# Moving the norm sums, the GpSimd passes and the attention transposes of a two-block fp32 network on one Trainium2 core

## The chip, the cores and the metric

The kernel runs on one core of one Trainium2 chip. The metric is the device time of one execution in microseconds (us), from the first to the last instruction with what the runtime adds around it. TensorE does the matrix products (its weight loads are listed apart, as PEld), VectorE (DVE) and ScalarE (ACT) do elementwise work and reads of PSUM, GpSimd (POOL) does some elementwise passes that touch no PSUM, and SyncE (SP) starts most of the DMAs.

## What is computed

Two blocks run on a sequence of 512 tokens of width 1024, in fp32. The first block is a mixer (a gated MLP branch and a linear recurrence with forget gates, called HGRN2, joined by gates and an output product), followed by a feed-forward part with squared ReLU. The second block has two layers; each is a gated feed-forward part (GLU), a mixer, and another GLU. The mixer of layer 0 is differential attention beside a multiscale pool, the mixer of layer 1 is a short causal convolution. Each part begins with a norm over the 1024 features of a token:

```python
def rmsnorm_2(x, g):
    xf = x.astype(jnp.float32)
    y = xf * lax.rsqrt(jnp.mean(xf * xf, axis=-1, keepdims=True) + EPS)
    return (y * g.astype(jnp.float32)).astype(x.dtype)

def modulated_norm(x, g, shift, scale):
    return rmsnorm_2(x, g) * (1 + scale) + shift

def swiglu(h, wg, wu, wd):
    return (jax.nn.silu(h @ wg) * (h @ wu)) @ wd
```

The shift and scale of the second block come from a vector `c` through a large matrix `w_ada` (72 DMAs of 1 MB). One norm, after the first block, is two norms in a row (its final norm and the first norm of the second block).

## The kernel before, in words

**Layout.** Activations are kept with the features on the 128 partitions and the tokens along the free axis: x is eight tiles of 128x512 (`xs(m)`). A product in fp32 is made of three passes in the faster format fp32r (`mm3`, L135): each operand is split into a high and a low part (`split`, L201; `wblock`, L119, for weights: ACT writes `whi` at L128, DVE writes `wlo` at L129), and high by high, high by low and low by high are added in PSUM (L139, L140, L141). Weights come in 1 MB DMAs on SP's queue; two landing buffers and four pairs of `whi`/`wlo` are in rotation.

**A norm between two parts.** `down` (L291) makes the last product of a part, feature tile by feature tile. After each tile it updates x on DVE (L300 or L298), squares it on ACT (L220) and adds the square into the sum `SS` (L226; on POOL for all tiles but the last). For the last two tiles (m = 6 and 7) the tokens go in two halves of 256. From here on the order of TensorE's instructions is the written one (`order_pe`), to the end of the next part's first products (`free_pe`); the other engines are ordered by the scheduler when the kernel is built. `norm_parts` (L249) gives two pieces per half. `sums` adds over the partitions with a matmul (L232), makes mean plus epsilon on DVE (L94) and raises it to -1/2 on POOL (L95). `tiles` spreads the 256 results over all partitions (`bcast`, L97) and then makes the eight normed tiles: `ht` on DVE (L270), its high part on ACT (L274 or L277), its low part on DVE (L275 or L278). `bcast` splits the two columns into high and low (L100, L101, both DVE), writes them into a diagonal matrix (L104, DVE, 512 columns for the two parts) and multiplies it by ones (L111, two fp32r matmuls of 256 columns).

In the order of TensorE the first half's `sums` stand just after the product of tile 6, second half; then comes the product of tile 7, second half, and the first half's spread stands three of its steps before the end:

```python
        finish(6, self.gemm([ws[0]], xs, 256, 256)[0], 1)
        parts[0][0]()
        n = len(xs)
        ps = self.acc()
        for k in range(n):
            if k == n - 3 and pre is None:
                parts[0][1]()
            self.mm3(ps, ws[1], k, xs[k], 256, 256, k == 0, k == n - 1)
```

In the double norm (`pre`) both sums are taken and the spread comes after the whole product. There are seven such norms; six of them are plain.

**First products of a part.** `lead_gemm` (L363) multiplies the first half of the tokens by four weight units at once, so that each normed tile feeds 12 matmuls of 256 columns; after the second and the fifth tile it puts the second half's `sums` and spread (`pump`). `lead_second` (L372) then does the second half, two units at a time. This is used by the feed-forward with ReLU, by four GLUs and by the convolution (L1084); attention has its own form by tokens (`gemm_tok_halves`, L180).

**Other passes on POOL.** The sums of squares of the first norm (L403), the affine part of a layer norm (L671, L672), the sum of the two gated branches (L539), the output gate of the recurrence (L642), the windows of the pool (L919) and the first tap of the convolution (L1097). The small powers (L95) are on POOL too.

**Attention.** `attn` (L809) makes q and k by tokens, norms them per head (`qk_evac`: square on ACT, L853 and L856 on DVE, power on POOL) and turns them (`finish`, L868 transposes). Then 16 steps run (token block i, head h), each in stages that belong to different steps: stA scores and exponentials, stB two steps later (difference of the two softmaxes, transposes at L984), stC three steps later (product with v at L993, norm, L996, L95, L999), stD four steps later (transpose at L1006, write of `oT`). Between the stages TensorE is filled with products for v and for the pool (`fill`), and after the last step with the beginning of the output product (`opening`), which needs the pool's results `pT`. `pool_out` multiplies a pool window by a 128x128 matrix that POOL's queue loads just before (L941, L942). The order of TensorE is the written one here too.

## Time and profile before

| | us |
|---|---|
| three runs | 2772.61, 2772.81, 2776.55 |
| median | 2772.81 |
| profiled execution | 2773.61 |
| its span | 2771.8 |
| mean granted TensorE clock | 0.991 of 2.4 GHz |

In a row of the timeline stand the start, the duration, the engine, the source line, the operation, what is written from what, the number of merged instructions, and in brackets how long the engine had been idle and for what. A matmul's duration holds its passage through the array, which overlaps the next one; how long a matmul costs is read from the distance of two starts. "PE acc L140 <- DVE h L275" says that a matmul of L140 waited for the DVE instruction of L275.

### The profile page before, as it was taken

To read this page: it belongs to the slowest core of one execution; us is meant where nothing else is said; L and a number is where in the kernel's file an instruction comes from. 1 tells how busy PE (TensorE), PEld (TensorE's weight loads), DVE (VectorE), ACT (ScalarE), POOL (GpSimd) and SP (SyncE) were. 2 spreads that over 40 slices of the span, in tenths; PEclk is the share of its full clock that TensorE was granted. 3 is DMA by queue.
4 is the path that set the end of the run, shared out by engine and by line. 5 is a ranking of instruction groups with operands and counts; after the bars stand their busy time and mean duration, and the time that the engine had idled before them with its cause. 6 is when DMAs were issued, how large, how long until landed. Compare 5 with 4: busy or idle time off the path is not lost.

```text
span 2771.8 us, 32091 instructions
## 1 busy us (share of the span) xinstructions
PE 2709.4 (98%) x13188; PEld 2279.7 (82%) x13188; DVE 1417.9 (51%) x2220; ACT 857.1 (31%) x1279; POOL 222.5 (8%) x205
## 2 busy tenths in 40 slices
PE   8999999999999899999989999999999999999999
PEld 6888888888888788887768888888888888888888
DVE  7566643476556755557567333354333354533333
ACT  5222232333224322224444222233222332332221
POOL 3000010200002000002221000010000111100000
PEclk9999999999999999999999999999999999999999
DMA  4211133355555455543223222322323222232222
GB/s 156 77 63 59 39 122 107 115 199 188 198 191 183 151 193 199 197 180 129 77 79 137 92 101 89 103 88 92 106 84 107 99 77 94 89 107 92 99 102 73
DMA packets 51266, 327.97 MB, mean 118 GB/s; under 512 B 5824, under 2 KB 6464, under 8 KB 17072
## 3 DMA queue, kind: packets, MB, share of 16 engines
q1 hardware_dynamic: 50256, 323.11, 33.0%
q0 software_dynamic: 864, 2.82, 0.3%
q8 instruction: 103, 1.69, 0.2%
q14 instruction: 43, 0.35, 0.0%
HBM read 323.81 MB, written 2.10 MB: 118 GB/s over the span
## 4 chain that ended last, share of the span: by engine, by line
PE 88%; DVE 6%; DMA 3%; issue 1%; POOL 1%; ACT 1%; SPq 0%; DVEq 0%; POOLq 0%; ACTq 0%
PE acc L140 26%; PE acc L141 26%; PE acc L139 26%; DMA ada<-in_w_ada 2%; PE ms L585 2%; DVE ada L784 1%; DVE wlo L129 1%; PE acc L172 1%; PE acc L173 1%; PE acc L171 1%; PE ms L623 1%; PE acc L199 0%; PE acc L197 0%; PE acc L198 0%; PE ms L111 0%
## 5 line engine op out<-in xcount | busy, mean ns | idle before, releaser
L128 ACT CAST whi<-w 128x1024 fp32r<-128x1024 f32 (+1 forms) x468 | 481.9, 1030 | 1517.5 <-PE acc L140 1407.5
L139 PE MATMUL acc<-h,whi 128*128 128x512 f32 (+1 forms) x2352 | 892.9, 380 | 3.8 <-ACT h L277 2.5
L140 PE MATMUL acc<-h,whi 128*128 128x512 f32 (+1 forms) x2352 | 887.4, 377 | 3.5 <-DVE h L275 2.6
L141 PE MATMUL acc<-h,wlo 128*128 128x512 f32 (+1 forms) x2352 | 885.9, 377 | 1.1 <-DVE wlo L129 1.1
L129 DVE TENSOR_TENSOR wlo<-w,whi 128x1024 fp32r<-128x1024 f32 (+1 forms) x468 | 573.4, 1226 | 447.5 <-ACT whi L128 439.0
L140 PEld LDWEIGHTS acc<-h,whi 128*128 128x128 f32 x2352 | 446.8, 190 | 83.8 <-DVE h L275 3.4
L139 PEld LDWEIGHTS acc<-h,whi 128*128 128x128 f32 x2352 | 446.9, 190 | 83.2 <-ACT h L277 3.6
L141 PEld LDWEIGHTS acc<-h,wlo 128*128 128x128 f32 x2352 | 446.4, 190 | 79.4 <-DVE wlo L129 1.7
L139 PE MATMUL acc<-y,whi 128*128 128x512 f32 (+1 forms) x1112 | 415.0, 373 | 1.0 <-ACT y L204 1.0
L140 PE MATMUL acc<-y,whi 128*128 128x512 f32 (+1 forms) x1112 | 414.8, 373 | 1.1 <-DVE y L205 1.1
L141 PE MATMUL acc<-y,wlo 128*128 128x512 f32 (+1 forms) x1112 | 414.7, 373 | 0.0
L784 DVE SCALAR_TENSOR_TENSOR ada<-ada,cb 128x1024 f32<-128x1024 f32 x144 | 181.6, 1267 | 118.6 <-DMA ada<-in_w_ada 118.2
L140 PEld LDWEIGHTS acc<-y,whi 128*128 128x128 f32 x1112 | 209.7, 189 | 38.4 <-DVE y L205 1.8
L139 PEld LDWEIGHTS acc<-y,whi 128*128 128x128 f32 x1112 | 209.7, 189 | 38.0 <-ACT y L204 1.4
L141 PEld LDWEIGHTS acc<-y,wlo 128*128 128x128 f32 x1112 | 209.7, 189 | 36.3
L300 DVE SCALAR_TENSOR_TENSOR xt<-acc,dmod,xt 128x512 f32<-128x512 f32 (+1 forms) x124 | 86.6, 698 | 261.4 <-PE acc L141 261.3
L764 DVE TENSOR_TENSOR e<-acc,e 128x512 f32<-128x512 f32 (+1 forms) x92 | 60.4, 656 | 233.3 <-PE acc L141 232.9
L204 ACT CAST y<-e 128x512 fp32r<-128x512 f32 (+1 forms) x140 | 81.6, 584 | 69.2 <-DVE e L749 38.4
L205 DVE TENSOR_TENSOR y<-e,y 128x512 fp32r<-128x512 f32 (+1 forms) x140 | 89.5, 640 | 11.0 <-ACT y L204 10.9
L223 POOL COPY SS<-sq 128x512 f32<-128x512 f32 x8 | 7.2, 912 | 995.6 <-ACT sq L220 995.6
L226 POOL TENSOR_TENSOR SS<-SS,sq 128x512 f32<-128x512 f32 x40 | 63.9, 1601 | 109.6 <-ACT sq L220 107.6
L277 ACT ACTIVATE h<-ht,mod 128x256 fp32r<-128x256 f32 x96 | 44.6, 502 | 75.3 <-DVE ht L270 75.3
(268 smaller groups left out, 2234.7 us busy)
## 6 DMA issues: line engine op xcount, KB each, us to landing
w<-in_w_gu SPq DMA_DIRECT2D x88, 1024.0 KB, 4.8
ada<-in_w_ada SPq DMA_DIRECT2D x72, 1024.0 KB, 6.3
w<-in_w_ff SPq DMA_DIRECT2D x32, 1024.0 KB, 4.8
w<-in_w_dn SPq DMA_DIRECT2D x32, 896.0 KB, 4.6
w<-in_w_dn SPq DMA_DIRECT2D x16, 1024.0 KB, 4.8
w<-in_w_fq SPq DMA_DIRECT2D x8, 1024.0 KB, 4.7
w<-in_w_gg SPq DMA_DIRECT2D x8, 1024.0 KB, 5.7
w<-in_w_cx SPq DMA_DIRECT2D x8, 1024.0 KB, 4.8
```

Source lines behind the costliest of these rows:

```text
L128: nc.scalar.copy(hi[:, :n], w[:, o:o + n])
L129: nc.vector.tensor_tensor(out=lo[:, :n], in0=w[:, o:o + n], in1=hi[:, :n].bitcast(F32), op=ALU.subtract)
L139: nc.tensor.matmul(o, lhsT=hi[:, k, :], rhs=x[:, 0, t0:t0 + tn], start=first, stop=False)
L140: nc.tensor.matmul(o, lhsT=hi[:, k, :], rhs=x[:, 1, t0:t0 + tn], start=False, stop=False)
L141: nc.tensor.matmul(o, lhsT=lo[:, k, :], rhs=x[:, 0, t0:t0 + tn], start=False, stop=last)
L204: nc.scalar.copy(h, src)
L205: nc.vector.tensor_tensor(out=dst[:, 1, t0:t0 + tn], in0=src, in1=h.bitcast(F32), op=ALU.subtract)
L226: eng.tensor_tensor(out=dst, in0=dst, in1=sq, op=ALU.add)
L300: nc.vector.scalar_tensor_tensor(out=x, in0=ps[:, :tn], scalar=gcol[:, m:m + 1], in1=x, op0=ALU.mult, op1=ALU.add)
L585: nc.tensor.matmul(ps[:, c * 64:(c + 1) * 64].rearrange("p (n b) -> p n b", b=b), lhsT=K[:, s], rhs=half(Q[:, s], 1), start=True, stop=True)
L764: nc.vector.tensor_tensor(out=y, in0=pss[1][:, :tn], in1=t, op=ALU.mult)
L784: nc.vector.scalar_tensor_tensor(out=w[:, i, :], in0=w[:, i, :], scalar=1.0, in1=cb, op0=ALU.mult, op1=ALU.mult, accum_out=self.mod[l][:, ...
```

## The change

It does eight things. `bcast` for two columns writes one diagonal of 256 columns in fp32 and spreads it with one fp32 matmul; for four columns the copy into the high part moves from DVE to ACT. The passes of L226, L403, L539, L642, L671, L672, L919 and L1097 move from POOL to DVE. In `down` the first half's `sums` move into the product of tile 6, second half, two steps before its end. `lead_gemm` and `lead_second` become `lead`: three units on the first half, then the fourth unit, then the second half in two pairs; each result is read out as soon as its group is done. In attention the q transposes stand after the second step of the k product, the k transposes of the first token block after four steps of filling, and those of the other three blocks in the steps 1 to 3. `stD` comes five steps after stA, with one more iteration. `opening` runs over all four output tiles with two pool groups before it turns to the other two, and the last `pool_out` comes one iteration later. The four pool matrices are loaded once, on SP's queue, into the free tile `SS2`.

```diff
     def bcast(self, dst, r, n):
+        idb = self.ident.rearrange("p (a o n) -> p a o n", a=1, o=1)
+        if n == 2:
+            dg = self.wk("diag", (128, 2, 2, 128), 1, F32R)[:, 0].bitcast(F32)
+            nc.vector.tensor_tensor(
+                out=dg, in0=idb[:, 0].to_broadcast([128, 2, 128]),
+                in1=r.rearrange("p (n o) -> p n o", o=1).to_broadcast([128, 2, 128]), op=ALU.mult)
+            nc.tensor.matmul(dst, lhsT=self.ones, rhs=dg.rearrange("p n c -> p (n c)"), start=True, stop=True)
+            return
-        nc.vector.tensor_copy(rs[:, 0, :n], r)
+        nc.scalar.copy(rs[:, 0, :n], r)
...
-        eng = nc.vector if m == 7 else nc.gpsimd
-        eng.tensor_tensor(out=dst, in0=dst, in1=sq, op=ALU.add)
+        nc.vector.tensor_tensor(out=dst, in0=dst, in1=sq, op=ALU.add)
...
-        finish(6, self.gemm([ws[0]], xs, 256, 256)[0], 1)
-        parts[0][0]()
         n = len(xs)
+        ps = self.acc()
+        for k in range(n):
+            if k == n - 2:
+                parts[0][0]()
+            self.mm3(ps, ws[0], k, xs[k], 256, 256, k == 0, k == n - 1)
+        finish(6, ps, 1)
...
+    def lead(self, wus, hs, done):
+        for c, (part, t0) in enumerate((((0, 1, 2), 0), ((3,), 0), ((0, 1), 256), ((2, 3), 256))):
+            pss = [self.ms() if c == 2 and j else self.acc() for j in part]
+            for k in range(8):
+                for ps, j in zip(pss, part):
+                    self.mm3(ps, wus[j], k, hs[k], t0, 256, k == 0, k == 7)
+                if c == 0 and k in (2, 6):
+                    self.pump()
+            for ps, j in zip(pss, part):
+                done(j, ps, t0)
...
-            for tb in range(4):
-                next(gk)
-                fq(tb)
+            next(gk)
+            next(gk)
+            fq(0)
+            fq(1)
+            next(gk)
+            fq(2)
+            next(gk)
+            fq(3)
...
+            pw = self.SS2.rearrange("p (g n) -> p g n", g=4)
+            nc.sync.dma_start(out=pw, in_=a["pool_w"])
...
-                pw = ap.tile([128, 128], F32, tag="poolw", name="poolw", bufs=1)
-                nc.gpsimd.dma_start(out=pw, in_=a["pool_w"][:, g, :])
-                nc.tensor.matmul(py, lhsT=pw, rhs=dvs.pop(g), start=True, stop=True)
+                nc.tensor.matmul(py, lhsT=pw[:, g, :], rhs=dvs.pop(g), start=True, stop=True)
...
-            for tb in range(4):
+            for _ in range(4):
                 next(fill)
-                fk(tb)
+            fk(0)
...
-            for s in range(ns + 4):
+            for s in range(ns + 5):
                 f = fill if s < ns else tailf
+                if s in (1, 2, 3):
+                    fk(s)
...
-                elif s == ns:
+                elif s == ns + 1:
                     pool_out(0)
...
-                if 0 <= s - 4 < ns:
-                    stD(*steps[s - 4])
+                if 0 <= s - 5 < ns:
+                    stD(*steps[s - 5])
```

The other moved passes change `nc.gpsimd` to `nc.vector` in one word each.

## Rows read from the trace of the kernel before

**Rows 1.** The page: busy time of two engines, share of the span, instructions

```profile
PE 2709.4 (98%) x13188; PEld 2279.7 (82%) x13188; DVE 1417.9 (51%) x2220; ACT 857.1 (31%) x1279; POOL 222.5 (8%) x205
```

**Rows 2.** What PE waited for: us in total, times, longest us

```profile
PE ms L111 <- DVE diag L104: 22.6, 11, 6.3
...
PE acc L172 <- DVE wlo L129: 4.2, 1, 4.2
PE ms L868 <- DVE qn L862: 3.8, 1, 3.8
PE ms L942 <- DMA poolw<-in_pool_w: 3.0, 1, 3.0
PE acc L140 <- DVE h L275: 2.6, 3, 1.5
...
PE ms L1006 <- DVE ht L999: 1.9, 1, 1.9
...
PE acc L140 <- DVE pT L946: 1.0, 1, 1.0
```

**Rows 3.** Timeline of PE, DVE and POOL, one plain norm (before a GLU)

```profile
1850.52 0.28 PE L139 MATMUL acc<-y,whi 128*128 128x256 f32 x1
1850.64 0.28 PE L140 MATMUL acc<-y,whi 128*128 128x256 f32 x1
...
1851.24 0.50 PE L232 MATMUL ms<-ones_r,SS 128*128 128x1 f32 x4
...
1852.06 0.71 POOL L95 TENSOR_TENSOR r<-rs_t,mhalf 128x2 f32<-128x2 f32 x1 [3.85 <-DVE rs_t L94]
...
1852.80 0.72 DVE L100 CAST rsp<-r 128x2 fp32r<-128x2 f32 x1 [0.82 <-POOL r L95]
...
1853.43 1.21 DVE L129 TENSOR_TENSOR wlo<-w,whi 128x1024 fp32r<-128x1024 f32 x1
...
1854.75 0.69 DVE L104 TENSOR_TENSOR diag<-ident,rsp 128x512 fp32r<-128x512 f32 x1
...
1855.50 0.50 PE L111 MATMUL ms<-diag,ones_r 128*128 128x256 f32 x2 [2.23 <-DVE diag L104]
```

**Rows 4.** Timeline of PE and DVE, the double norm

```profile
903.61 1.02 PE L232 MATMUL ms<-ones_r,SS 128*128 128x1 f32 x8
...
908.56 0.16 DVE L262 TENSOR_TENSOR r<-r 128x2 f32<-128x2 f32 x1 [0.82 <-POOL r L95]
...
913.94 0.80 PE L111 MATMUL ms<-diag,ones_r 128*128 128x256 f32 x2 [6.34 <-DVE diag L104]
```

**Rows 5.** Groups by line and shape: busy us, mean ns, idle before

```profile
L226 POOL TENSOR_TENSOR SS<-SS,sq 128x512 f32<-128x512 f32 x40 | 63.9, 1601 | 109.6 <-ACT sq L220 107.6 <-DMA ada<-in_w_ada 1.8
...
L226 DVE TENSOR_TENSOR SS<-SS,sqh 128x256 f32<-128x256 f32 x16 | 6.8, 437 | 3.9 <-ACT sqh L220 3.9
...
L278 DVE SCALAR_TENSOR_TENSOR h<-ht,mod,h 128x256 fp32r<-128x256 f32 x96 | 44.3, 495 | 3.5 <-ACT h L277 3.0
...
L270 DVE SCALAR_TENSOR_TENSOR ht<-xt,dmod,ms 128x256 f32<-128x256 f32 x80 | 35.9, 487 | 5.5 <-PE ms L111 5.5
```

**Rows 6.** Timeline of PE in attention, fp32 matmuls of 512 columns

```profile
1405.55 1.88 PE L965 MATMUL acc<-kT,qz 128*128 128x512 f32 x4
1406.87 0.79 PE L139 MATMUL acc<-h,whi 128*128 128x512 f32 x1
1407.50 0.39 PE L140 MATMUL acc<-h,whi 128*128 128x512 f32 x1
```

**Rows 7.** Timeline of DVE in the first mixer, with POOL busy and idle

```profile
46.98 4.58 DVE L205 TENSOR_TENSOR h<-e,h 128x512 fp32r<-128x512 f32 x3
...
60.31 0.68 DVE L205 TENSOR_TENSOR h<-e,h 128x512 fp32r<-128x512 f32 x1
```

**Rows 8.** Windows at half clock (one, and the sum of ten): us, busy time, PEclk

```profile
1856.40:1859.80 3.40, 3.40 (x17) 3.20 (x16) 3.21 (x7) 2.67 (x5) 0.00 (x0) 0.50 0.01 2
sum 47.60, PE 41.14 PEld 35.06 DVE 36.20 ACT 20.41 POOL 4.01; mean PE 4.11 PEld 3.51 DVE 3.62 ACT 2.04 POOL 0.40
```

More of the change, by code (lines that the diff above doesn't have):

```diff
@@ L402, in square @@
                 else:
-                    (nc.vector if m > 5 else nc.gpsimd).tensor_tensor(out=self.SS, in0=self.SS, in1=sq, op=ALU.add)
+                    nc.vector.tensor_tensor(out=self.SS, in0=self.SS, in1=sq, op=ALU.add)
             for m in range(8):
@@ L538, in mixer1 @@
                 nc.vector.tensor_tensor(out=u, in0=yb, in1=sb, op=ALU.mult)
-                nc.gpsimd.tensor_tensor(out=u, in0=u, in1=sa, op=ALU.add)
+                nc.vector.tensor_tensor(out=u, in0=u, in1=sa, op=ALU.add)
                 d = self.slot("mix", mp)
@@ L670, in gmlp @@
                                     op0=ALU.add, op1=ALU.mult)
-            nc.gpsimd.tensor_tensor(out=v, in0=v, in1=rows[:, 0, :], op=ALU.mult)
-            nc.gpsimd.tensor_tensor(out=v, in0=v, in1=rows[:, 1, :], op=ALU.add)
+            nc.vector.tensor_tensor(out=v, in0=v, in1=rows[:, 0, :], op=ALU.mult)
+            nc.vector.tensor_tensor(out=v, in0=v, in1=rows[:, 1, :], op=ALU.add)
         us = []
@@ L714, in ffn, with done @@
                 flat = [(w, ds[j // n]) for ws, ds in lead for j, w in enumerate(ws)]
-                pss = self.lead_gemm([f[0] for f in flat], hs)
-                for j in range(0, 4, n):
-                    evac(flat[j][1], pss[j:j + n], 0, 256)
-                for j in range(0, 4, 2):
-                    ps2 = self.lead_second([f[0] for f in flat[j:j + 2]], hs, j == 0)
-                    for i in range(0, 2, n):
-                        evac(flat[j + i][1], ps2[i:i + n], 256, 256)
+                got = {}
+                def done(j, ps, t0):
+                    got[j] = ps
+                    if j % n == n - 1:
+                        evac(flat[j][1], [got.pop(j - n + 1 + i) for i in range(n)], t0, 256)
+                self.lead([f[0] for f in flat], hs, done)
                 self.free_pe()
@@ L918, in window @@
                         dst = bufs[1 + j % 2]
-                        nc.gpsimd.tensor_tensor(out=dst[:, 16:528], in0=cur[:, 16:528],
+                        nc.vector.tensor_tensor(out=dst[:, 16:528], in0=cur[:, 16:528],
                                                 in1=cur[:, 16 - (1 << j):528 - (1 << j)], op=ALU.add)
@@ L1015, in opening @@
             def opening():
-                for m in range(4):
-                    if m % 2 == 0:
-                        wd[m // 2] = self.wblock(a["w_oab"][m // 2], [(8, 128)] * 2)
-                    ps = po_[m] = self.acc()
-                    for k in (7, 6, 5, 4):
-                        self.mm3(ps, wd[m // 2][m % 2], k, pT[k - 4], 0, 512, k == 7, False)
-                        if k % 2 == 0:
-                            yield
+                for ks in ((7, 6), (5, 4)):
+                    for m in range(4):
+                        if m not in po_:
+                            if m % 2 == 0:
+                                wd[m // 2] = self.wblock(a["w_oab"][m // 2], [(8, 128)] * 2)
+                            po_[m] = self.acc()
+                        for k in ks:
+                            self.mm3(po_[m], wd[m // 2][m % 2], k, pT[k - 4], 0, 512, k == 7, False)
+                        yield
             def closing(m):
@@ L1083, in conv, with done @@
                 vtile(i)
-            pss = self.lead_gemm(lead[0] + lead[1], hs)
-            for i in range(2):
-                gate_in(i, None, 0, 256, pss[2 * i:2 * i + 2])
-            for i in range(2):
-                gate_in(i, None, 256, 256, self.lead_second(lead[i], hs, i == 0))
+            got = {}
+            def done(j, ps, t0):
+                got[j] = ps
+                if j % 2:
+                    gate_in(j // 2, None, t0, 256, [got.pop(j - 1), got.pop(j)])
+            self.lead(lead[0] + lead[1], hs, done)
             self.free_pe()
```

21 lines of the change are left out of this document (3 added, 18 removed).

## The prediction, made before the change was run

> **What bounds the kernel now.** I read the page's first part first. TensorE is busy for 2709.4 of 2771.8 us, DVE for half of the span, POOL for 222.5 us [rows 1]. So only two things can pay: TensorE's 62 idle us, and time in which it works slowly. Work that leaves POOL, or comes to DVE, costs or gives nothing by itself. The second view is the list of what TensorE waited for; there the reader sees that the idle time has few owners [rows 2]: 22.6 us in eleven waits for the diagonal of a norm's spread, 4.2 us for a `wlo` in the first mixer, and in attention 3.8 us (k transposes), 3.0 us (DMA of the pool matrix), 1.9 us (stD's transpose) and 1.0 us (the last `pT`). The third view is the timeline of one plain norm [rows 3]. The fourth, the table of windows, shows what a wait costs beyond itself: ten stretches, most of them right behind such a wait, run at a granted clock of 0.50, the 1.2 GHz level. They last 47.6 us and TensorE is busy in 41.1 of them [rows 8]; at the full level that work would take half, so some 20 us are lost there.
>
> **The sum goes against the profiled execution**, 2773.61 us (span 2771.8). It lies 0.8 us above the median of 2772.81, which I take off at the end.
>
> **Plain norms (six).** From the sum matmul to the spread 4.26 us pass (1851.24 to 1855.50), and TensorE idles in 2.23 of them [rows 3]. The change takes out or moves: the sum stands two steps, six matmuls of 0.12 us, earlier (0.72); L100 (0.72) and L101 (as small as L262's 0.16 [rows 4]) go; the diagonal has 256 columns in place of 512, so 0.44 by a DVE pass of that width [rows 5] in place of 0.69. That is 1.8 us. It can be 3.0: the `wlo` pass of 1.21 us that sat between L100 and L104 [rows 3] no longer finds a pair of dependent passes to slip into, though the scheduler may put it ahead of the diagonal. A wait of about 2 us is thus nearly covered. Of the 22.6 us of rows 2, 6.3 are the double norm's; of the remaining 16.3 I take back 11.5 (bounds 6 and 14). What is late next is the first normed tile, below. The sum now stands close behind the add of tile 7's first half, on DVE in both kernels; nothing else is queued behind it on TensorE that could run.
>
> **Double norm (one).** 10.3 us pass from the sums to the spread, 6.34 of them idle, and 5.4 of them after the last power's result (L262) [rows 4]. There the queue of DVE holds `wlo` and `ada` passes of about 1.2 us between every two dependent small ones. One such hop in place of three remains: 1.2 + 0.44 and some 0.3 of hand-over, 3.4 us less; with the 0.72 of the earlier sum about 4 us, and 0.8 on the second half. I take -4.8 (bounds -2 and -6).
>
> **Spread in fp32.** Four fp32 records of 512 columns and one fp32r matmul of 512 take 1.95 us between L965 and L140 [rows 6]. With 0.24 for the fp32r one (twice the 0.12 of 256 columns [rows 3]) a record costs 0.43; two records make one fp32 matmul, so 0.86 for 512 columns and 0.43 for 256. The old pair takes 2 x 0.12 [rows 3]. There are 16 spreads of two columns (seven norms, two halves, and two for `scale`): 16 x 0.19 = **+3.0**. For four columns L100 moves to ACT; no row has so small an ACT copy, and it goes between 0 and +0.5 a time on a path that no wait of rows 2 owns: 0.
>
> **Attention.** The waits of rows 2 are 3.8 + 3.0 + 1.9 + 1.0 = 9.7 us, and each loses its cause: four fill steps (24 matmuls of 0.24, 5.8 us) stand before the first k transposes; the four pool matrices come once on SP, 256 KB long before they are read, so the four POOL DMAs go and SP's weight loads are pushed back by one short transfer; stD is a step later; the last pool group is needed four matmul groups later. The extra iteration holds stD alone, with the same two fill steps before it. Against it, ten window adds come to DVE, 10 x 0.69, in a stage where its passes sit between TensorE's. I take **-9** (bounds -4 and -12; beyond 9.7 lie shorter waits).
>
> **Clock.** Of the ten slow stretches [rows 8] seven lie behind waits that I expect to go or to shrink; each costs 1.7 us (3.4 at half rate). If half of that is won, **-6** (bounds 0 and -13).
>
> **First mixer and the moved passes.** `wlo` is 4.2 us late there [rows 2] because DVE is. Beside the POOL passes L671 and L672 three L205 take 4.58 us; one alone takes 0.68 [rows 7], so 2.5 us of DVE were lost in those three, and some 5.5 in the whole stretch by the same rate. The eight passes that come to DVE cost 8 x 0.68 = 5.4. I take 0 (bounds -4 and +5). Of this the Trainium skill says, on the page GPSIMD Engine Reference (1, Specifications), that POOL shares its SBUF interfaces with VectorE, with contention for DVE passes that have two SBUF inputs or run in a two-port mode. The trace agrees for L205, with its 2.5 us; by that rule a moved pass pays back only where such DVE passes ran beside it, and with no payback the stretch would end 5.4 us later. In the rest of the run the 40 adds of L226 take 64 us on POOL [rows 5] and 40 x 0.69 on DVE, and the other moved passes about as much again, some 65 us in all on an engine with 1350 idle: 0, as long as they don't stand before a pass that TensorE waits for; the bound is +4.
>
> **First products, three wide (six parts).** A normed tile costs DVE 0.49 + 0.50 us [rows 5]. Four-wide, TensorE eats one in 12 x 0.12 = 1.44 us, three-wide in 1.08. Over eight tiles DVE's slack shrinks from 3.7 to 0.8 us, and at least a `wlo` pass (1.21), the x update (0.5) and an add (0.44) fall into it, 2.1 us. So 1.3 us become waits; a start with three `wlo` passes in place of four gives some back. I take 1.0 a part, **+6** (bounds -2 and +15). It is the largest single doubt.
>
> **Sum:** -11.5 - 4.8 + 3.0 - 9 - 6 + 0 + 6 = -22.3, so 2751.3 against the profiled execution, 2750.5 against the median.
>
> **The rivals.** (a) *More is won*: the fourth `wlo` was what held up the first products, the clock stays up, and the first mixer gains. Then the lead term is 0 (6 us better), the clock -11 (5 better), the norms -13 (1.5 better) and the first mixer -1: -22.3 - 13.5 = -35.8, or 2737. For it speaks that a wait for a `wlo` or a normed tile follows most norms; against it the 0.8 us of slack. (b) *The waits move on*: the spread comes earlier, but the first tile and its low part do not follow because DVE has the same passes to do; norms -4, double norm -2, attention -6, clock -2, +3, +6: -5, 2768. For it speak the 2.6 us that TensorE already waits for the low part of a tile [rows 2]. That the change doesn't do what it says belongs here: the order on DVE is the scheduler's, and an unlucky `wlo` in the chain gives 1.2 us of each norm back. (c) *Slower*: the lead starves. Place: the six three-wide products; price: each DVE pass that falls in front of a tile's own is a TensorE wait, 1.2 us for a `wlo` or `ada` pass, and a slow stretch like those of rows 8 behind it costs 1.7 more. It decides from about 5.7 us a part, three or four such passes and one slow stretch: (5.7 - 1.0) x 6 = 28 eats the -22. At 6.5 a part the time is about 2783. Against it: in the double norm, with four `ada` and `wlo` passes in the way, most of that delay came before the spread, not behind it. Beside this stands a sentence of the Trainium skill, TensorE: Matmul & The Clock Gate (Part 1, engine queue depths), that DVE's queue is strictly first in, first out; in the trace an L129 of 1.21 us starts ahead of the L104 that TensorE waits for [rows 3], which agrees.
>
> **How the numbers follow.** Chances: forecast 0.52, (a) 0.25, (b) 0.16, (c) 0.07. The forecast's own range is 2740 to 2762. Holding eight in ten means taking in (a) and most of (b): 2731 to 2767. About 0.2%, 5.5 us, is what a measurement of this kernel can tell from no change; (b) lies on that edge, so half of it counts as the same: faster 0.85, same 0.09, slower 0.06.
>
> **What would show it.** Right: the wait for L111's diagonal falls from 22.6 to some 8 us; the four attention waits are gone; fewer than six half-clock stretches; L111's successor at 0.43 us. Wrong: new waits of `acc` for `h` or `wlo` of over 10 us in all behind the norms (then (b) or (c)); a `wlo` wait in the first mixer above 6 us; in attention waits for stB's or stC's DVE passes. A TensorE busy time that grows by more than 3 us would say that the spread was mis-sized.

## The result and the profile after

The changed kernel takes 2740.24 us (median of four runs, 2739.53 to 2742.72), against 2772.71 for the kernel before beside it: a ratio of 0.9881, 95% interval 0.9864 to 0.9898, so 32.5 us less. The forecast was 2750.5 with a range of 2731 to 2767. The sign and the range held; the sum was 10 us short.

The profiled execution took 2739.53 us, its span is 2737.4. Most lines move by 6 to 11: L104 and L111 are now L102 and L105 for two columns and L112 and L118 for four, L139 to L141 are L146 to L148, L226 is L232, L232 is L238, L270 is L276, L274/L275 and L277/L278 are L280/L281 and L283/L284.

The page's first part, busy time of the engines [rows 1]:

```profile
PE 2696.5 (99%) x13188; PEld 2273.0 (83%) x13188; DVE 1425.5 (52%) x2282; ACT 856.5 (31%) x1288; POOL 69.0 (3%) x98
```

TensorE's idle time (span less busy) went from 62.4 to 40.9 us, and its busy time fell by 12.9 us with the same 13188 matmuls. The second cannot be fewer waits: it is for the most part work done at a higher clock. The windows of the four stretches at half clock inside the kernel say so (their sum; columns as in [rows 8]):

```profile
sum 17.00, PE 15.49 PEld 13.96 DVE 14.88 ACT 4.63 POOL 0.00; mean PE 3.87 PEld 3.49 DVE 3.72 ACT 1.16 POOL 0.00
```

Before, TensorE was busy in 41.1 us of such time [rows 8], now in 15.5; at the full level the difference takes half, so 12.8 us came back. What TensorE waits for now, behind its 6.9 us for the first weights at the start (us in total, times, longest):

```profile
PE acc L146 <- ACT h L283: 5.4, 5, 2.0
PE acc L147 <- DVE h L284: 5.1, 6, 1.3
PE acc L146 <- ACT h L280: 3.6, 2, 3.5
PE acc L147 <- DVE h L281: 3.3, 4, 2.1
PE acc L179 <- DVE wlo L136: 2.8, 1, 2.8
PE ms L1004 <- ACT awT L997: 2.2, 1, 2.2
PE ms L1017 <- DVE ht L1010: 1.4, 1, 1.4
PE acc L204 <- ACT h L283: 1.4, 1, 1.4
PE ms L105 <- DVE mod L802: 0.8, 1, 0.8
PE ms L118 <- DVE diag L112: 0.8, 1, 0.8
```

The 22.6 us for the diagonal [rows 2] are all but gone. In their place stand 18.8 us for the normed tiles (the five rows with `h`), of which there were 7.0 before. One plain norm shows how (timeline, the norm of [rows 3]):

```profile
1819.46 0.52 PE L238 MATMUL ms<-ones_r,SS 128*128 128x1 f32 x4
...
1820.99 0.43 DVE L102 TENSOR_TENSOR diag<-ident,r 128x256 f32<-128x256 f32 x1 [0.81 <-POOL r L95]
...
1821.33 0.48 DVE L306 SCALAR_TENSOR_TENSOR xt<-acc,dmod,xt 128x256 f32<-128x256 f32 x1
...
1821.80 1.23 DVE L136 TENSOR_TENSOR wlo<-w,whi 128x1024 fp32r<-128x1024 f32 x1
...
1822.07 0.60 PE L105 MATMUL ms<-diag,ones_r 128*128 128x256 f32 x2
...
1822.94 0.42 DVE L232 TENSOR_TENSOR SS<-SS,sqh 128x256 f32<-128x256 f32 x1
...
1823.28 0.87 DVE L276 SCALAR_TENSOR_TENSOR ht<-xt,dmod,ms 128x256 f32<-128x256 f32 x2
...
1825.15 0.38 PE L146 MATMUL acc<-h,whi 128*128 128x256 f32 x1 [1.43 <-ACT h L283]
...
1826.40 0.39 PE L147 MATMUL acc<-h,whi 128*128 128x256 f32 x1 [0.86 <-DVE h L284]
```

The spread starts without a wait. Then the first `ht` stands in DVE's queue behind `xt`, `wlo` and the add, and TensorE waits 1.43 and 0.86 us for its two parts: nearly the 2.23 us that it waited for the spread before.

The same norms mark stages that can be compared between kernels. The table gives the time from one norm's first sum matmul to the next, and in its last row to the last matmul (start times in the timeline), of one profiled execution each. The columns with single parts are explained with the runs; in the changed kernel and in the norm edits the earlier sum takes 0.7 us from the first stage and gives it to the last.

| stage | before | moved passes alone | norm edits alone | attention's order alone | changed |
|---|---|---|---|---|---|
| first mixer | 541.1 | 531.8 | 540.9 | 539.4 | 534.1 |
| ReLU feed-forward | 362.5 | 361.5 | 362.9 | 362.6 | 363.6 |
| double norm, GLU | 380.4 | 373.7 | 374.8 | 380.5 | 370.9 |
| attention | 196.6 | 191.2 | 194.7 | 189.3 | 184.5 |
| GLU | 370.6 | 371.3 | 366.2 | 370.7 | 366.3 |
| GLU | 366.7 | 366.3 | 364.8 | 366.6 | 365.7 |
| convolution | 181.3 | 182.0 | 179.5 | 181.3 | 180.5 |
| GLU to the end | 368.9 | 368.7 | 368.0 | 368.9 | 368.2 |

A stage is good to about 1.7 us: the first mixer, of which attention's order changes nothing, is 1.7 us shorter in that run, 0.8 of it ahead of its first sum and the rest where one stretch at half clock came shorter. The double norm's stage is less sure: with the same code there e4_attn has 371.5 us and e7_cb 375.6 (the wait near 1120 us, told with f1_copy). Of the 34 us, 7.0 came from the first mixer, 9.5 from the double norm and its GLU, 12.1 from attention with its norm, 4.3 from the GLU behind it, and under one from each later norm. The ReLU part lost 1.1.

### The profile page after: what moved, and what is told of

It is laid out like the page before. It is cut to its first block, busy times and chain, and to the rows that moved or that the text cites. A ratio compares the mean times of both kernels' runs of the same rounds, so it can differ in the third digit from the quotient of the medians.

```text
span 2737.4 us, 32001 instructions
## 1 busy us (share of the span) xinstructions
PE 2696.5 (99%) x13188; PEld 2273.0 (83%) x13188; DVE 1425.5 (52%) x2282; ACT 856.5 (31%) x1288; POOL 69.0 (3%) x98
## 4 chain that ended last, share of the span: by engine, by line
PE 90%; DVE 5%; DMA 2%; issue 1%; ACT 1%; POOL 1%; SPq 0%; DVEq 0%; POOLq 0%; ACTq 0%
PE acc L147 27%; PE acc L146 27%; PE acc L148 27%; PE ms L590 2%; DMA ada<-in_w_ada 1%; DVE wlo L136 1%; PE acc L179 1%; PE acc L180 1%; PE acc L178 1%; DVE ada L790 1%; PE ms L628 1%; PE acc L206 1%; PE acc L205 1%; PE acc L204 0%; PE ms L568 0%
## 5 line engine op out<-in xcount | busy, mean ns | idle before, releaser
L146 PE MATMUL acc<-h,whi 128*128 128x512 f32 (+1 forms) x2352 | 891.6, 379 | 9.0 <-ACT h L283 5.4
L148 PE MATMUL acc<-h,wlo 128*128 128x512 f32 (+1 forms) x2352 | 883.5, 376 | 0.0
L136 DVE TENSOR_TENSOR wlo<-w,whi 128x1024 fp32r<-128x1024 f32 (+1 forms) x468 | 559.9, 1197 | 460.4 <-ACT whi L135 449.0
L146 PEld LDWEIGHTS acc<-h,whi 128*128 128x128 f32 x2352 | 445.1, 189 | 88.8 <-ACT h L283 6.6
L148 PEld LDWEIGHTS acc<-h,wlo 128*128 128x128 f32 x2352 | 445.1, 189 | 77.5
L146 PE MATMUL acc<-y,whi 128*128 128x512 f32 (+1 forms) x1112 | 415.5, 374 | 0.0
L148 PE MATMUL acc<-y,wlo 128*128 128x512 f32 (+1 forms) x1112 | 414.4, 373 | 0.0
L146 PEld LDWEIGHTS acc<-y,whi 128*128 128x128 f32 x1112 | 209.6, 188 | 36.8
L148 PEld LDWEIGHTS acc<-y,wlo 128*128 128x128 f32 x1112 | 209.5, 188 | 36.3
L790 DVE SCALAR_TENSOR_TENSOR ada<-ada,cb 128x1024 f32<-128x1024 f32 x144 | 174.8, 1222 | 105.9 <-DMA ada<-in_w_ada 105.8
L590 PEld LDWEIGHTS ms<-kq 128*128 128x128 f32 x448 | 56.3, 192 | 3.1
L283 ACT ACTIVATE h<-ht,mod 128x256 fp32r<-128x256 f32 x96 | 44.0, 502 | 45.6 <-DVE ht L276 45.6
L304 DVE TENSOR_TENSOR xt<-xt,acc 128x512 f32<-128x512 f32 (+1 forms) x44 | 28.0, 637 | 55.6 <-PE acc L148 55.6
```

Source lines behind the costliest of these rows:

```text
L136: nc.vector.tensor_tensor(out=lo[:, :n], in0=w[:, o:o + n], in1=hi[:, :n].bitcast(F32), op=ALU.subtract)
L146: nc.tensor.matmul(o, lhsT=hi[:, k, :], rhs=x[:, 0, t0:t0 + tn], start=first, stop=False)
L148: nc.tensor.matmul(o, lhsT=lo[:, k, :], rhs=x[:, 0, t0:t0 + tn], start=False, stop=last)
L283: nc.scalar.activation(out=h, in_=t, func=AF.Identity, bias=shcols[:, k:k + 1])
L590: nc.tensor.matmul(ps[:, c * 64:(c + 1) * 64].rearrange("p (n b) -> p n b", b=b), lhsT=K[:, s], rhs=half(Q[:, s], 1), start=True, stop=True)
L790: nc.vector.scalar_tensor_tensor(out=w[:, i, :], in0=w[:, i, :], scalar=1.0, in1=cb, op0=ALU.mult, op1=ALU.mult, accum_out=self.mod[l][:, ...
```

## The experiments

### The parts undone in the changed kernel, one at a time

The kernel before took 2776.09 us beside the first four of these and 2773.89 beside the fifth, against 2772.71 beside the changed kernel. So ratios are compared with the 0.9881, not times; 0.001 is 2.8 us.

**e1_spread.** The two-column spread as before.

```diff
-        if n == 2:
+        if n == 1:
```

> The changed kernel with one part undone: the two-column spread is again the split into high and low, a diagonal of 512 columns on DVE and two fp32r matmuls of 256 columns. The changed kernel stands at 0.9881 of the kernel before (2740.2 us). Theory 1, the short chain is what covers the spread's wait: the two DVE passes and the wider diagonal come back into the chain between power and spread (some 1.1 us, more where a wlo pass of 1.2 us slips between them), the waits for the diagonal come back in part (from under 2 us in all to 8 to 12), and with two or three stretches at half clock the time is 8 to 15 us longer, less 3 us for the cheaper spread: 5 to 12 us slower than the changed kernel, ratio 0.990 to 0.9925. Theory 2, the move of the sum by six matmuls and the relief of DVE's order alone cover the wait and the chain has slack: the fp32 spread only costs its 16 x 0.19 = 3 us on TensorE, and the time falls by 0 to 3 us: ratio 0.987 to 0.988.

Measured: 2744.18 us, ratio 0.9889 (0.9870 to 0.9907). That is 2.2 us more than the changed kernel, in neither theory's range, and the intervals overlap. By the waits theory 1 holds in small: the diagonal (L118) costs 4.2 us in three waits, and the waits for `h` stay (19.6 us in six rows). The short chain is worth a little; it is not what carries the gain.

**e2_pool.** All moved passes back on POOL.

```diff
-        nc.vector.tensor_tensor(out=dst, in0=dst, in1=sq, op=ALU.add)
+        eng = nc.vector if m == 7 else nc.gpsimd
+        eng.tensor_tensor(out=dst, in0=dst, in1=sq, op=ALU.add)
...
-            nc.vector.tensor_tensor(out=v, in0=v, in1=rows[:, 0, :], op=ALU.mult)
-            nc.vector.tensor_tensor(out=v, in0=v, in1=rows[:, 1, :], op=ALU.add)
+            nc.gpsimd.tensor_tensor(out=v, in0=v, in1=rows[:, 0, :], op=ALU.mult)
+            nc.gpsimd.tensor_tensor(out=v, in0=v, in1=rows[:, 1, :], op=ALU.add)
```

> The changed kernel with one part undone: every elementwise pass that came to DVE (squares' sums, first norm's sums, gated sum, output gate, affine part of the layer norm, pool windows, first tap of the convolution) is on POOL again; the sums of the last tile's halves for m = 7 stay on DVE as before. Theory 1, these passes only matter where TensorE waits for DVE beside them, the first mixer and attention: 2 to 6 us slower than the changed kernel (ratio 0.989 to 0.990), with the first mixer's wait for wlo back from 2.8 to about 4.2 us and the norm waits where they are. Theory 2, relief of DVE from POOL's passes shortens the norms' chains too (the last add of tile 6 on POOL takes 0.9 us or more against 0.44 on DVE, and DVE passes beside POOL are slowed): 10 to 18 us slower, ratio 0.992 to 0.995, with waits for the diagonal back. Theory 3, nothing: within 2 us.

Measured: 2750.56 us, ratio 0.9908 (0.9893 to 0.9923): 7.5 us slower than the changed kernel by the ratios, between theories 1 and 2; its lowest time, 2747.97, lies above the changed kernel's highest, though the two intervals overlap by 0.0005. The first mixer ends at 541.0 us, where it ended before, and its wait is back:

```profile
PE acc L179 <- DVE wlo L136: 5.7, 1, 5.7
```

The waits for the diagonal do not come back (1.1 us). A part that the prediction had put at 0 is the largest of the undone ones.

**e3_four.** First products four wide again.

```diff
-        for c, (part, t0) in enumerate((((0, 1, 2), 0), ((3,), 0), ((0, 1), 256), ((2, 3), 256))):
-            pss = [self.ms() if c == 2 and j else self.acc() for j in part]
+        for c, (part, t0) in enumerate((((0, 1, 2, 3), 0), ((0, 1), 256), ((2, 3), 256))):
+            pss = [self.ms() if c == 1 and j else self.acc() for j in part]
...
-                if c == 0 and k in (2, 6):
+                if c == 0 and k in (1, 4):
```

> The changed kernel with one part undone: the first products of a part are four units wide again on the first half of the tokens (second half's sums and spread behind the second and fifth tile), the rest of the change stays. My prediction gave the three-wide form a cost of 1.0 us a part, because each tile feeds 9 matmuls in place of 12. If that holds, this kernel is 3 to 8 us faster than the changed one (ratio 0.985 to 0.987), and the waits for h (17.4 us in the changed kernel) fall by half. Rival: the fourth unit's wlo was what held up the first products, and the three-wide start gains: this kernel is 4 to 10 us slower (ratio 0.9895 to 0.992), with waits for wlo in the first products. Third case: DVE makes up for it in either form, within 2 us.

Measured: 2742.44 us, ratio 0.9880 (0.9865 to 0.9894): the same as the changed kernel. The waits show that both views were half right. Those for `h` fall to 16.1 us (five rows), and a new one for the fourth unit's low part stands in the list:

```profile
PE acc L148 <- DVE wlo L136: 5.2, 3, 4.8
```

**e4_attn.** Attention's order as before, the pool windows on DVE.

```diff
-            for s in range(ns + 5):
+            for s in range(ns + 4):
...
-                if 0 <= s - 5 < ns:
-                    stD(*steps[s - 5])
+                if 0 <= s - 4 < ns:
+                    stD(*steps[s - 4])
```

and the transposes, `opening`, `pool_out` and the pool matrices likewise.

> The changed kernel with one part undone: all of attention's order is as before (q transposes one behind each step of the k product, k transposes one behind each of the first four fill steps, the last stage four steps behind the first, the opening one output tile after the other, the last pool product one iteration earlier, the four pool matrices loaded by POOL's queue just before their use); the pool windows stay on DVE. Theory, as in the prediction: the four waits come back, 9.7 us, less the 3.6 us of waits that the changed kernel has in their place, and with two stretches at half clock of 1.7 us each: 8 to 13 us slower, ratio 0.991 to 0.993. Rival, waits there are caught up by the weights or tiles that TensorE would wait for next: under 4 us, ratio under 0.9896.

Measured: 2744.10 us, ratio 0.9889 (0.9873 to 0.9906): 2.2 us slower, a quarter of the theory's least and inside the rival's range; attention's stage of the profiled execution is 4.1 us longer (188.6 against 184.5). The old waits are back, without the 1.9 us of stD's transpose:

```profile
PE ms L874 <- DVE qn L868: 3.8, 1, 3.8
...
PE ms L948 <- DMA poolw<-in_pool_w: 2.6, 1, 2.6
...
PE acc L147 <- DVE pT L952: 1.2, 1, 1.2
```

**e5_sums.** The first half's sum six matmuls later.

```diff
-            if k == n - 2:
-                parts[0][0]()
...
         finish(6, ps, 1)
+        parts[0][0]()
```

> The changed kernel with one part undone: the first half's sums stand again behind the whole product of tile 6, second half, six matmuls of 0.12 us later. Theory 1, the chain of the changed kernel just fits: the spread in the changed kernel starts without a wait, with about 0.5 us to spare, so 0.2 to 0.7 us come back in each of seven norms, and with one or two stretches at half clock of 1.7 us: 2 to 7 us slower than the changed kernel (ratio 0.989 to 0.9905), the waits for the diagonal 2 to 5 us in all. Theory 2, the spread is not what is late now but the first normed tile behind DVE's queue, so nothing comes back: within 2 us.

Measured: 2744.17 us, ratio 0.9892 (0.9877 to 0.9907). The four times run from 2740.97 to 2748.15, so the 3.0 us by the ratios are not settled. The waits for the diagonal are 2.2 us in all (1.5 and 0.7), the lower end of theory 1.

### The parts alone in the kernel before

Undone one at a time the parts give back 2.2 + 7.5 + 0 + 2.2 + 3.0 = 15 us of 32.5, and only the moved passes' share stands clear of the scatter of times. If two parts remove the same wait, undoing one shows little. So each group was put alone into the kernel before.

**a1_pool.** The moved passes alone (e2_pool's edit the other way).

> The kernel before with one part of the change alone: every elementwise pass that the change takes from POOL is on DVE, nothing else is changed. Undoing this part in the changed kernel cost about 10 us, of which 7 lie in the first mixer (its end at 541.0 us as before, against 534.1) and 4 in attention; my prediction gave the moved passes 0 (bounds -4 and +5). Theory 1, the gain stands by itself: 9 to 13 us faster than before (ratio 0.9953 to 0.9968), the first mixer ends at 534 to 535 us, attention (the first sum of its norm to the first sum behind it) falls from 186 to about 182. Theory 2, it pays only beside the shorter chains of the norms: 2 to 6 us faster (ratio over 0.998), the first mixer ends after 538 us. In either case the waits for the diagonal of the spread stay near 22.6 us, save for the last add of tile 6 that comes earlier (at most 1 us a norm).

Measured: 2751.87 us against 2773.89, ratio 0.9921 (0.9906 to 0.9935): 22.0 us faster, twice theory 1. The first mixer ends at 531.8 us. Waits of this kernel:

```profile
PE ms L111 <- DVE diag L104: 16.4, 10, 2.7
...
PE acc L172 <- DVE wlo L129: 1.3, 1, 1.3
```

The longest wait for a diagonal, the double norm's 6.3 us [rows 2], is at most 2.7 us here, with the chain as long as before. Why DVE gained is in the groups by line and shape, ahead the kernel before, then this one:

```profile
L129 DVE TENSOR_TENSOR wlo<-w,whi 128x1024 fp32r<-128x1024 f32 x396 | 497.0, 1256 | 400.6 <-ACT whi L128 393.6 <-PE acc L965 0.2
L784 DVE SCALAR_TENSOR_TENSOR ada<-ada,cb 128x1024 f32<-128x1024 f32 x144 | 181.6, 1267 | 118.6 <-DMA ada<-in_w_ada 118.2
L300 DVE SCALAR_TENSOR_TENSOR xt<-acc,dmod,xt 128x512 f32<-128x512 f32 x100 | 75.0, 750 | 237.8 <-PE acc L141 237.8
```

```profile
L129 DVE TENSOR_TENSOR wlo<-w,whi 128x1024 fp32r<-128x1024 f32 x396 | 483.5, 1223 | 413.0 <-ACT whi L128 405.4
L783 DVE SCALAR_TENSOR_TENSOR ada<-ada,cb 128x1024 f32<-128x1024 f32 x144 | 175.1, 1222 | 87.5 <-DMA ada<-in_w_ada 87.3
L299 DVE SCALAR_TENSOR_TENSOR xt<-acc,dmod,xt 128x512 f32<-128x512 f32 x100 | 75.0, 750 | 244.5 <-PE acc L141 244.5
```

With POOL out of the way the `wlo` passes lose 13.5 us and the `ada` passes 6.5, while the x update, with one operand in PSUM, keeps its 750 ns. One place where this reaches TensorE is the first mixer. There DVE's queue is full from the layer norm's first affine pass to the late `wlo` (timeline of DVE, the kernel before, then this one):

```profile
42.60 3.86 DVE L669 TENSOR_SCALAR gvl<-gvl,gst 128x512 f32<-128x512 f32 x4 [1.13 <-POOL gst L95]
...
51.48 5.18 DVE L438 SCALAR_TENSOR_TENSOR e<-xt,cols,grb 128x512 f32<-128x512 f32 x3
...
60.91 1.22 DVE L129 TENSOR_TENSOR wlo<-w,whi 128x1024 fp32r<-128x1024 f32 x1
```

```profile
40.97 1.00 DVE L668 TENSOR_SCALAR gvl<-gvl,gst 128x512 f32<-128x512 f32 x2 [1.13 <-POOL gst L95]
...
50.62 2.07 DVE L437 SCALAR_TENSOR_TENSOR e<-xt,cols,grb 128x512 f32<-128x512 f32 x3
...
56.34 1.22 DVE L129 TENSOR_TENSOR wlo<-w,whi 128x1024 fp32r<-128x1024 f32 x1
```

From the first row to the `wlo` 18.31 us pass before and 15.37 here, with eight passes more. Beside POOL's passes the four L669, the three L438 and three L205 [rows 7] took 3.86, 5.18 and 4.58 us; without them they take 2.00, 2.07 and some 1.9. So 7.7 us were lost, and the eight passes cost 4.8 (41.89 to 44.30 and 45.21 to 47.62). The difference, 2.9 us, is what the wait for `wlo` loses (4.2 to 1.3), and the 6.8 us at half clock behind it are gone too.

The double norm gains in another way. DVE behind the last power's result (L262 at 908.56 [rows 4], here L261), the kernel before, then this one:

```profile
908.64 1.22 DVE L784 SCALAR_TENSOR_TENSOR ada<-ada,cb 128x1024 f32<-128x1024 f32 x1
...
910.18 1.22 DVE L129 TENSOR_TENSOR wlo<-w,whi 128x1024 fp32r<-128x1024 f32 x1
...
913.20 0.69 DVE L104 TENSOR_TENSOR diag<-ident,rsp 128x512 fp32r<-128x512 f32 x1
```

```profile
897.93 0.16 DVE L261 TENSOR_TENSOR r<-r 128x2 f32<-128x2 f32 x1 [0.34 <-POOL r L95]
...
898.52 0.69 DVE L104 TENSOR_TENSOR diag<-ident,rsp 128x512 fp32r<-128x512 f32 x1
```

From the sum to that result both kernels need nearly the same, 4.95 and 4.72 us. From there to the diagonal it is 4.64 us before and 0.59 here: two matrix steps, a `wlo` pass and three smaller ones, none of them stretched, stood between the dependent passes, and here none does. That is the order in which the scheduler queued DVE's passes when the kernel was built. The edit changed it; that POOL slows DVE did not make this wait. In a3_norm, which keeps POOL's adds, the queue is also free of them, and sum to spread takes 4.60 us (903.73 to 908.33), as in the changed kernel (897.70 to 902.30).

Passes of that norm were stretched too (the kernel before, DVE and POOL), but without POOL's adds the chain to the power is only those 0.2 us shorter:

```profile
899.95 1.99 DVE L784 SCALAR_TENSOR_TENSOR ada<-ada,cb 128x1024 f32<-128x1024 f32 x1
...
905.14 1.43 POOL L226 TENSOR_TENSOR SS<-SS,sqh 128x256 f32<-128x256 f32 x2
...
905.20 0.69 DVE L259 TENSOR_TENSOR r<-r 128x2 f32<-128x2 f32 x1 [0.82 <-POOL r L95]
```

The matrix step takes 1.99 us for its usual 1.22, and a pass of two columns 0.69 for the 0.16 of L262 [rows 4]. On this the Trainium skill, SBUF — State Buffer (Who interferes with whom), says that a VectorE instruction with two SBUF inputs contends with a GpSimd instruction that reads SBUF, and that one with at most one SBUF input does not, outside the modes in which it uses two ports. The rows agree: `wlo`, `ada` and L259 are stretched, the x update is not. L669, with one tile as input, is stretched as well; no row shows in which mode it ran.

In attention the last stage's wait of 1.9 us [rows 2] is absent here and in e4_attn, where the windows are on DVE and the order is the old one, and there in a2_ssq and a3_norm, where they are on POOL.

**a2_ssq.** Of the moved passes only the adds of squares (L226).

```diff
-        eng = nc.vector if m == 7 else nc.gpsimd
-        eng.tensor_tensor(out=dst, in0=dst, in1=sq, op=ALU.add)
+        nc.vector.tensor_tensor(out=dst, in0=dst, in1=sq, op=ALU.add)
```

> The kernel before with only the adds of the squares (48 passes of 512 columns or a half) moved from POOL to DVE. All moved passes together gave 22 us against my 0; by the times of the norms' sums 9 of these lie in the first mixer, 7 in the double norm and the layer before it, 6 in attention. Theory 1, the adds own the double norm's share: there DVE's passes beside a POOL add are stretched (a matrix step 1.99 us for 1.22, a wlo 1.55, a small pass 0.69 for 0.16) and the last add of tile 6 ends late: 5 to 9 us faster than before (ratio 0.9968 to 0.998), all of it in the double norm and the GLU behind it, the first mixer unchanged, its end at 541 us. Theory 2, the double norm gained because the stage before it ended earlier and met the matrix DMAs at another moment: under 3 us.

Measured: 2766.17 us, ratio 0.9971 (0.9960 to 0.9981): 7.1 us faster, by 56 passes (2220 to 2276), not 48. The stage of the double norm falls by 5.6 us (380.4 to 374.8), which is theory 1's place but not its mechanism: here too the passes from L261 (905.95) to the diagonal (906.54) follow one another without a `wlo` or `ada` between them. The first mixer ends at 539.6, 1.5 us earlier, about what one shorter stretch at half clock gives, so most of the mixer's 9 us in a1_pool belong to its own passes.

**a3_norm.** The norms' edits alone: the changed kernel with both e2_pool's and e4_attn's edits.

> The kernel before with the norms' edits alone: short two-column spread in fp32, copy for four columns on ACT, the earlier first sum, and first products three wide; POOL's passes and attention's order are as before. My prediction's terms for these are -11.5 - 4.8 + 3.0 + 6 and some -4 of the clock, -11 in all: ratio 0.996, no less. By the undo runs (all edits but the moved passes 24 us faster than before, attention's order worth 4 to 5) it is 18 to 21 us faster: ratio 0.9925 to 0.9935. If the sum of the separate gains is more than the whole (32.5), the parts remove the same waits.

Measured: 2757.21 us, ratio 0.9941 (0.9929 to 0.9954): 16.1 us faster, between the prediction's 11 and the 18 to 21.

**a4_attn.** Attention's order alone (e4_attn's edit the other way, windows on POOL).

> The kernel before with attention's order alone (later transposes, the last stage five steps behind, the new opening, the pool matrices loaded once on SP's queue); the pool windows stay on POOL. My prediction's term is -9 and some -2 of the clock: ratio 0.996. Undone in the changed kernel it cost 4 us, since waits of 4.7 us in the third and last stage took the place of the 9.7: then it is 4 to 6 us faster, ratio 0.998 to 0.9986, with waits for awT, pT or ht of over 3 us in the steps. With POOL's windows in the way it can be less still.

Measured: 2765.68 us, ratio 0.9971 (0.9959 to 0.9982): 7.6 us faster, more than the 4 to 6 expected; 1.7 us of it lie in the first mixer, which the edit leaves alone. Three of the old waits are gone. The last stage's transpose (here L1011) still waits, 1.3 us at another step, and with three new waits that makes 5.9 us:

```profile
PE ms L998 <- DVE pT L951: 2.3, 1, 2.3
...
PE ms L989 <- DVE ht L1004: 1.5, 1, 1.5
...
PE ms L1011 <- DVE ht L1004: 1.3, 1, 1.3
...
PE ms L989 <- DVE oT L1015: 0.8, 1, 0.8
```

The three groups alone gain 22.0 + 16.1 + 7.6 = 45.7 us, together 32.5: 13 us do not add up. The table shows where: in the double norm's stage 6.7 and 5.6 alone, 9.5 together; in attention's 5.5, 1.9 and 7.3 alone, 12.1 together; in the first mixer 9.3, 0.2 and 1.7 alone, 7.0 together. In the double norm two parts remove the same wait; for the mixer see f1_copy.

### Tries to go further

**e6_early.** The first half's spread two steps earlier.

```diff
-            if k == n - 3 and pre is None:
+            if k == n - 5 and pre is None:
```

> The changed kernel with the first half's spread five steps before the end of the product of tile 7 instead of three (0.72 us earlier in the order). In the changed kernel TensorE waits 17.4 us for the normed tiles. Theory 1, these waits begin with the spread: the first tile comes up to 0.7 us earlier, less what the spread now waits for its diagonal: 1 to 4 us faster than the changed kernel. Theory 2, the first tile stands in DVE's queue behind the x update, a wlo pass of 1.2 us and the add, and the earlier spread only turns into a wait for the diagonal: 0 to 4 us slower, with waits for the diagonal of 2 to 5 us and the waits for the tiles unchanged.

Measured: 2742.57 us, ratio 0.9883 (0.9868 to 0.9898), no difference. The same norm in this kernel:

```profile
1820.07 0.52 PE L238 MATMUL ms<-ones_r,SS 128*128 128x1 f32 x4
...
1822.07 0.70 PE L105 MATMUL ms<-diag,ones_r 128*128 128x256 f32 x2
...
1823.88 0.87 DVE L276 SCALAR_TENSOR_TENSOR ht<-xt,dmod,ms 128x256 f32<-128x256 f32 x2
```

From the sum the spread comes after 2.00 us in place of 2.61, the first `ht` after 3.81 in place of 3.82. So the tile does not wait for the spread but for its turn on DVE, as theory 2 said; its waits for the diagonal did not come.

**e7_cb.** The activation of `c` deferred, in the ReLU feed-forward, where TensorE waits 3.5 us for one tile.

```diff
-        nc.scalar.activation(out=cb, in_=cb, func=AF.Silu)
+        self.ada_hold = True
+
+        def warm():
+            nc.scalar.activation(out=cb, in_=cb, func=AF.Silu)
+            self.ada_hold = False
+
+        self.late = [warm]
```

> The changed kernel with the activation of the vector c put after the first products of the feed-forward with ReLU (in the kernel it stands on ACT's queue just there and waits for its DMA), and the matrix steps for shift and scale with it. In the changed kernel TensorE stands still 3.6 and 2.4 us there and runs 6.8 us at half clock. Theory 1, the activation of c blocks ACT's queue in front of a normed tile: both waits go and with them the half clock, 6 + 3.4 us less, so 5 to 9 us faster than the changed kernel (ratio 0.985 to 0.986). Theory 2, the wait is the change of ACT's function table for that norm, or the tiles are late in DVE's queue anyway: within 2 us.

Measured: 2740.46 us, ratio 0.9876 (0.9860 to 0.9893), as the changed kernel. The edit did not do what it says: the scheduler put the activation back in its old place, ahead of the tile's high part (timeline of ACT):

```profile
544.57 1.28 ACT L784 ACT_TABLE_LOAD   x1 [4.23 <-DMA cb<-in_c_rep]
...
546.83 0.69 ACT L280 CAST h<-ht 128x256 fp32r<-128x256 f32 x2
```

ACT stands idle 4.23 us for the DMA of `c` with the tile behind it. That this is the cause of the 3.5 us wait is read from the row; removing it was not achieved.

**f1_copy.** The four-column copy back on DVE.

```diff
-        nc.scalar.copy(rs[:, 0, :n], r)
+        nc.vector.tensor_copy(rs[:, 0, :n], r)
```

> The changed kernel with the high-part copy of the four-column spread back on DVE. In the changed kernel the copy stands on ACT ahead of a table load of 1.28 us and of the gate's activations, the first mixer's wait for wlo is 2.8 us, with a stretch at half clock behind it; with the moved passes alone (copy on DVE) it is 1.3 us, without that stretch, and that part of the first mixer is 3.0 us shorter. Theory 1, the copy on ACT costs just that: 2 to 4 us faster than the changed kernel (ratio 0.9865 to 0.9875), the wait for wlo 1.3 us. Theory 2, the chain of the mixer is as late for another part of the change, or the 3 us are given back where a matrix DMA paces the first GLU: within 1.5 us.

Measured: 2738.28 us, ratio 0.9874 (0.9860 to 0.9887), the lowest of all, but the intervals do not part it from the changed kernel. The first mixer ends at 531.5 us, 2.5 earlier, with the wait for `wlo` at 1.3 us and no stretch at half clock behind it (e3_four and e6_early have none either, with 2.8 us of wait); attention's stage is 2.7 us shorter, as in e6_early (1.9) and e3_four (3.3) with the copy on ACT. The double norm's stage is 4.2 us longer, with a new wait:

```profile
PE acc L146 <- ACT y L211: 2.0, 1, 2.0
```

Ahead of it, on DVE:

```profile
1118.07 1.23 DVE L790 SCALAR_TENSOR_TENSOR ada<-ada,cb 128x1024 f32<-128x1024 f32 x1 [5.46 <-DMA ada<-in_w_ada]
...
1119.22 0.69 DVE L770 TENSOR_TENSOR e<-acc,e 128x512 f32<-128x512 f32 x1
```

DVE waits 5.46 us for a 1 MB matrix while the last tile of the GLU's middle product stands behind it. Theory 1 holds for the mixer. Whether the longer stage is theory 2's give-back is open: the changed kernel and e4_attn pass this place without the wait, e7_cb and e6_early, with the copy on ACT, have 1.2 and 1.1 us of it.

## Why the prediction was right, and where its sum was off

**Plain and double norms, first products: the idle time was right, in part by luck.** My terms for TensorE's idle time here were -11.5, -4.8 and +6, -10.3 in all; a3_norm's idle time is 62.4 - 50.6 = 11.8 us lower. Two errors met in it: the diagonal's waits fell by some 21 us where my terms had 16.3, and the waits for tiles rose by 11.8 where I had 6. The cause of the +6 was half right. Waits for tiles rose from 7.0 to 18.8 us, by rival (b)'s mechanism (DVE has the same passes to do), and my own sign of a wrong forecast, over 10 us of new ones, came true. The diagonal's waits fell to under 2 us where I had left 8. That the three-wide form costs 6 us is not borne out: four wide saves 2.7 us of tile waits and pays 5.2 for the fourth `wlo`, rival (a)'s mechanism.

**Clock: too small.** "If half of that is won, -6". Of the some 20 us lost there 12.8 came back. Busy time fell by 12.9 where my terms (+3.0 and -6) made 3.0; these 9.9 us are most of the difference between the span's 34.4 and my 22.3. By the windows' 12.8 less the spread's 3.0 it would be 9.8; the other 3.1 us of busy time are not explained. The step that failed is taking half of a price that hangs on each wait: when nearly all waits in front of the stretches shrink, most stretches go.

**Moved passes: the wrong step.** "Work that leaves POOL, or comes to DVE, costs or gives nothing by itself", and "First mixer and the moved passes ... 0 (bounds -4 and +5)". Alone they are worth 22.0 us, undone 7.5. For the first mixer the mechanism was in hand (2.5 us of DVE lost in three passes [rows 7]) and the sizes were off: I set 5.5 us lost against 5.4 for the passes that come, the runs show 7.7 against 4.8, and the 6.8 us at half clock behind the wait were not in the term. For the norms the term was nothing because DVE is idle for half of the span. Yet the L100 of 0.72 us that I charged to a plain norm's chain [rows 3] takes 0.17 in a1_pool: most of it was POOL's add beside it. This gave the plain norms little, since the add (0.42) now stands in DVE's queue (4.26 to 4.05 us from sum to spread). In the double norm I had named the owner, the passes queued between the dependent ones, but booked its removal under the shorter spread alone; moving the adds changes the same queue, and its wait falls from 6.34 to 2.14 us without the shorter spread. So the moved passes undone cost little beyond the mixer, which ends 6.9 us later (534.1 to 541.0). What was missing in the sum stayed unseen because the parts share waits: the whole's idle time fell by 21.5 us, my terms gave 19.3, the three groups alone 14.1 + 11.8 + 4.6 = 30.5.

**Attention: -9 was too much.** Three of the four waits lost their causes, as said; the last stage's transpose, a step later, still waits 1.4 us where it waited 1.9, and other waits stand close behind: a4_attn's idle time is 4.6 us lower, and its busy time 4.4. The whole of 7.6 us is inside my -4 to -12 by way of the clock.

**Spread in fp32.** From L105's start to that of the second matmul behind it the changed kernel's timeline has 0.55 us (1822.07 to 1822.62), 0.12 of them the first's: 0.43, as estimated. The sixteen of them are 3 us that the clock's gain hides.

**The rivals.** The time lies at the edge of the forecast's own range (2740 to 2762), nearer to (a)'s 2737 than to 2750.5. Of (a) the clock's part came, -11 as it had it, the fourth `wlo`, and a gain in the first mixer, larger than its 1 us; of (b) the mechanism without the time; (c), the starving lead, did not come: no wait for a tile exceeds 3.5 us, and that one is ACT's wait for the DMA of `c`.

**Still open:** how much of the short chain, the earlier sum and the three-wide form each holds, since their undo runs (0 to 3 us) lie within one another's intervals; what in attention sets the last stage free when the windows are on DVE; and why the place before 1120 us is passed with and without a wait.

## What to carry to other kernels

Before a pass is priced at nothing because its engine is idle, look at what it does to its neighbour: take one instruction's duration with and without the other engine at work, and ask whether the stretched ones stand in front of a pass that the busy engine waits for; then set what they lose against what the moved passes cost there. An edit that moves passes also changes the order in which the scheduler queues the others, so compare the queue in both kernels before a gain is put down to speed. Price the clock with the waits, wait by wait, and expect edits that shorten the same chain to overlap; run each alone as well as undone, since either by itself tells only half. A wait that vanishes names its successor in the in-order queue: read that queue up to the next instruction that the busy engine needs.

## What was not expected of the hardware

A DVE pass of two columns took 0.69 us beside a POOL add, four times its 0.16; a matrix step 1.99 for 1.22; 103 passes more on DVE (2220 to 2323) raised its busy time by only 18.2 us (1417.9 to 1436.1), where some 65 were expected by the 683 ns of an add of 512 columns in a1_pool. The same add took 1601 ns on POOL [rows 5]. And the clock came back by much more than the share of the waits removed: idle time fell by a third (62.4 to 40.9 us), time at half clock by nearly two thirds (47.6 to 17.0).
